# RWKV-7 scan of a two-layer diffusion block: groups of two chunks in place of four, two of them prepared at a time in each direction

## The chip, the cores and the metric

One core of a Trainium2 chip runs the whole program: two layers, one launch. The metric is the device time of an execution in microseconds (us), lower is better. TensorE is PE in the profile, VectorE DVE, ScalarE ACT, GpSimd POOL, and SyncE, which issues most DMAs, SP.

## The reference

Each layer normalizes 512 latent and 256 context tokens, projects them into four groups of mixers (HGRN2, RWKV-7, windowed attention, latent attention), joins them in an output projection and ends with a feed-forward part. The change concerns the RWKV-7 mixer alone, four heads of 64, a recurrence run once forwards and once backwards, over the context first and then over the latent tokens from the state that the context left:

```python
def rwkv7_scan(r, w, k, v, kk, b, s0, reverse):
    def step(S, inp):
        r_t, w_t, k_t, v_t, kk_t, b_t = inp
        sa = jnp.einsum('bhvk,bhk->bhv', S, kk_t)
        S = S * w_t[:, :, None, :] - sa[..., None] * b_t[:, :, None, :] + v_t[..., None] * k_t[:, :, None, :]
        return S, jnp.einsum('bhvk,bhk->bhv', S, r_t)
    xs = tuple(a.transpose(1, 0, 2, 3) for a in (r, w, k, v, kk, b))
    S, o = lax.scan(step, s0, xs, reverse=reverse)
    return o.transpose(1, 0, 2, 3), S

oc_f, sc_f = rwkv7_scan(rc, wc[0], kc, vc, kkc, bc, s0, False)
ol_f, _ = rwkv7_scan(rl, wl[0], kl, vl, kkl, bl, sc_f, False)
oc_b, sc_b = rwkv7_scan(rc, wc[1], kc, vc, kkc, bc, s0, True)
ol_b, _ = rwkv7_scan(rl, wl[1], kl, vl, kkl, bl, sc_b, True)
```

In the last layer the outputs of the context tokens are not needed, only their state.

## The kernel before, in words

The kernel doesn't go token by token. It takes chunks of 64 tokens, 12 in all (8 to 11 are the context, and come first in both directions). Within a chunk, what one token's update does to later ones is a triangular matrix, and the chunk needs its inverse. That inverse, and everything else that doesn't depend on the incoming state, can be made ahead for several chunks; only the state chain goes chunk after chunk.

`rw_dir` (L648) is the generator of one direction. It runs three groups of four chunks. `rw_quad` (L711) prepares a group: it loads the decays W and the keys kkq, makes the operands AR (zeroed halves, L740, then products with W, L741 to L744) and BK (L735, L736), multiplies them into the Gram blocks G for each chunk and masks them (L754), starts the inverse TT as mask plus identity (L763, L766), turns it (TU, TP), turns BK (bkt, L782), and then doubles the size of the inverted blocks in five levels. Each level has three steps with a `yield` behind each: a product of TP with the masked Gram block Gm (L786, on POOL) whose result goes to AP in two halves, one copied by DVE and one by ACT (`pad`, L633); a product of AP with TT, added into TU by DVE (L810) and copied to TP by ACT (L814); and a turn of TU on PE (L328), copied to TT by ACT (L820). The PE products of all helpers stand on L638 (`flip`) and L328 (`turn`).

`rw_chain` (L823) carries the state Z over one chunk: four groups of products (with v, AR·Z, TF, bkt and G), each followed by a copy or an addition on DVE or ACT; it writes the chunk's output into O (L863, L865).

The order of the work is that of the generators: `weave` takes one step of every live generator in turn, both directions, the attention's preparation (`attention_prep`, L1442, half a step at a time) and, in layer 0, the modulation (L425 to L437). Within a direction the group i+1 is prepared step by step beside the chain of group i; the first is prepared alone. Direction 1 starts 10 rounds later. Each engine runs its own instructions in the order so written.

Buffers set a further order. PSUM has two buffers of one bank per direction for the preparation (tag a0 or a1) and one for the chain (c0, c1). In SBUF, G and bkt have two buffers and AR three, all shared by the two directions; v (`vq`), TP and AP exist once per direction.

Of the kernel before, what the change touches and what calls it, by code (L numbers as in the profile page):

```python
# [11 lines left out]
F32 = mybir.dt.float32  # L12
# [5 lines left out]
OP = mybir.AluOpType  # L18
# [204 lines left out]
class Ker:  # L223
# [423 lines left out]

    def rw_dir(s, d, last, g, O, done, both, t0, tp):  # L648
        V = s.V
        s.bp = tp  # L650
# [8 lines left out]
        def values(i):  # L659
            lo = min(order[4 * i:4 * i + 4])  # L660
            for t in range(2):
                h = slice(64 * t, 64 * t + 64)
                s.Q.dma_start(vq[h, :, :, t], s.vd[h, lo:lo + 4].rearrange("p c (h n) -> p c h n", h=2))
        for n, sh in (('TP', [128, 8, 2, 64]), ('AP', [128, 8, 2, 32])):
            z[n], = s.zeroed(tp, sh, f"{n}{d}")
# [12 lines left out]

        def chain(i, Z, zi, ops):
            quad = order[4 * i:4 * i + 4]  # L680
            lo = min(quad)
            for c in range(4):
                Z = yield from s.rw_chain(d, lo, quad[c], last, g, O, done, tp, zi, ops, Z, i == 2 and c == 3)
            if not (last and lo >= 8):
                if lo in both:
                    s.head_squares(O, 1, lo, lo + 4, t0.tile([128, 4, 2, 64], F32, name="Wi"))
                both.add(lo)
            if i < 2:
                values(i + 1)
            return Z  # L690

        cur = yield from prep(0)
        for i in range(3):
            live = {'Z': chain(i, Z, *cur)}
            if i < 2:
                live['cur'] = prep(i + 1)
            res = {}
            while live:
                for n in list(live):
                    try:  # L700
                        next(live[n])
                    except StopIteration as e:
                        res[n] = e.value
                        del live[n]
                yield
            Z, cur = res['Z'], res.get('cur')
            s.rdone += i == 1

    def rw_quad(s, d, lo, last, g, tp, z):

        E, V, S, P = s.E, s.V, s.S, s.P  # L711
        o = 64 * lo
        want = not (last and lo >= 8)
        nm = f"{d}"

        def psa():
            return s.ps("a" + nm, 512, 2)

        def v(x):
            return x[:, :, o:o + 256].rearrange("p t (c n) -> p t c n", c=4)  # L720
        W = tp.tile([128, 2, 4, 64], F32, name="W", bufs=2)
        Wi = tp.tile([128, 2, 4, 64], F32, name="Wi")

# [3 lines left out]
        e = 0 if d else 63  # L727
        We = tp.tile([128, 2, 4, 1], F32, name="We" + nm, bufs=2)
        P.tensor_copy(We, W[:, :, :, e:e + 1])
        AR = z['AR']  # L730
        BK = (s.bp if d else tp).tile([128, 4, 2, 2, 64], F32, name="BK" + nm)
        kv, rv = tp.tile([128, 2, 4, 64], F32, name="kkq", bufs=2), v(g['r'])
        s.Q.dma_start(kv, v(s.rd[:, :2]))
# [11 lines left out]
        yield  # L745
        tp, TP, AP = s.bp, z['TP'], z['AP']
        na = 2 if want else 1

        G = tp.tile([128, 4, 2, 2, 2, 64], F32, name="G", bufs=2)
        for c in range(4):  # L750
# [5 lines left out]
            if c % 2:  # L756
                yield
        S0 = tp.tile([128, 4, 2, 64], F32, name="TT" + nm)

        for t in range(2):  # L760
            for p in range(2):
                h = slice(64 * t, 64 * t + 64)
                (V, P)[p].tensor_tensor(S0[64 * p:64 * p + 64, :, t], G[h, :, 0, p, 0],  # L763
                                s.mskf[h, 1 - d, 0][:, None].to_broadcast([64, 4, 64]), OP.mult)
        sh = [128, 4, 2, 64]
        V.tensor_add(S0, S0, s.id2[:, None, None].to_broadcast(sh))  # L766
        TT = S0
        pt = psa().rearrange("p (x n) -> p x n", x=8)
        for c in range(4):
            s.turn(pt[:, 2 * c:2 * c + 2], S0[:, c])  # L770
        TU = tp.tile([128, 8, 64], F32, name="TU" + nm)
# [5 lines left out]
        for c2 in range(2):  # L777
            pb = psa().rearrange("p (c q h n) -> p c q h n", c=2, q=2, h=2)
            for c in range(2):
                for q in range(2):  # L780
                    s.turn(pb[:, c, q], BK[:, 2 * c2 + c, q])
            S.copy(bkt[:, 2 * c2:2 * c2 + 2], pb)  # L782
        yield
# [5 lines left out]
        for i in range(1, 6):  # L789
            gm, h = gms[i], LVL[i]  # L790
            if i < 5:
                gms[i + 1] = masked(i + 1)

            def half(x):

                return x.rearrange("p x (b e h) -> p x b e h", e=2, h=h)[:, :, :, d]

            def packed(ps):
                return ps[:, :256].rearrange("p (x b h) -> p x b h", x=8, h=h)
            ps = psa()  # L800
            pa = packed(ps)
            for c in range(4):
                s.flip(pa[:, 2 * c:2 * c + 2], lambda p: gm[:, c, p], lambda p: half(TP[:, 2 * c + p]))
            s.pad(AP, ps[:, :256].rearrange("p (x n) -> p x n", x=8), 2)
            yield
            ps = psa()
            p2 = packed(ps)
            for c in range(4):
# [7 lines left out]
            pt = psa().rearrange("p (c t n) -> p c t n", c=4, t=2)  # L816
            for c in range(4):
# [485 lines left out]
    def mixers(s, l, last, xsrc):  # L1303
        V, S, P, Q = s.V, s.S, s.P, s.Q
# [5 lines left out]
        with ExitStack() as wx, ExitStack() as hx:  # L1310
# [7 lines left out]
            with ExitStack() as rx:  # L1318
                rp = rx.enter_context(s.pool("rec", side="right"))
                g = {}  # L1320
# [3 lines left out]
                with ExitStack() as ax:  # L1324
# [11 lines left out]
                    with s.pool("pr", 1, PSUM) as s.pp:  # L1336
# [89 lines left out]
                        done = set()  # L1426
# [15 lines left out]
                def attention_prep(psf):  # L1442
# [13 lines left out]
                    yield from s.swa_prep(l, last, sq, sk, qp, cst, psf, scr)  # L1456
                    while s.rdone < 2:
                        yield

# [4 lines left out]
                with s.pool("b") as tp, s.pool("pb", 1, PSUM) as s.pp:  # L1464
                    done = set(), set()
                    s.rdone, s.nhg = 0, 2
                    wq, wk = bp.tile([128, 768], F32, name="wq"), []
# [5 lines left out]
                    Q.dma_start(s.mskf, s.I['cst'][:, C_MSK:C_MSK + 768].rearrange("p (d h n) -> p d h n", d=2, h=6))  # L1473
                    s.weave(*((s.rw_dir(d, last, g, rwt, *done, tp, tp), 1) for d in range(2)),
                            (attention_prep(s.hps), 0.5), *modulation(tp, scr))
# [526 lines left out]
```

## Time and profile before

| | us |
|---|---|
| median of 3 runs (lowest to highest) | 2707.03 (2705.91 to 2714.2) |
| the profiled execution | 2717.58 |
| its span, mean granted TensorE clock | 2715.7, 0.949 |
| scan stage of layer 0, from 375.2 to 612.2 | 237.0 |
| scan stage of layer 1, from 1698.2 to 1914.5 | 216.3 |

All rows below come from the profiled execution; a time such as 391.16 is counted from the start of its span. The stages' borders are the end of the projection before them and the first product of the attention behind them.

How to read it: the page gives shares over the whole span, and the scan is a sixth of that, so the views of use are the windows (busy time of each engine in a stretch), the groups of instructions within a window (count, busy time, mean, and the idle time of the engine ahead of the group with what ended it), and timelines. "[13.33 <-POOL AR L744]" behind a row says that the engine had been idle for 13.33 us and that POOL's instruction of line 744, which writes AR, ended it. A profile row counts each PE product of the program as two matmuls.

### The profile page before, as it was taken

The numbers are of one execution on the slowest core, as the hardware profiler recorded it, in microseconds if no ns is written. First come the engines' busy times: TensorE is split into PE (matmuls) and PEld (weight loads), VectorE is DVE, ScalarE is ACT, GpSimd is POOL, SyncE is SP. The second block draws the span as 40 slices with busy tenths as digits, with TensorE's granted clock in tenths as the row PEclk, the third lists the DMA queues.
The fourth block names the chain that finished last, engine by engine and source line by source line (L and its number), as shares of the span: only waits on it lengthen the run. The fifth ranks groups of instructions, "written<-read, shape, count | busy, mean of one in ns | idle before, by whom it ended". The sixth has DMA issues, their size and how long they took to land. (4 is left out here: it accounts for less than half of the span.)

```text
span 2715.7 us, 45812 instructions
## 1 busy us (share of the span) xinstructions
PE 2423.3 (89%) x18131; PEld 2004.2 (74%) x18131; DVE 1642.9 (60%) x2846; ACT 1204.1 (44%) x2079; POOL 462.2 (17%) x477
## 2 busy tenths in 40 slices
PE   7998778879998999999999998687898799999994
PEld 3887555666577888888878867466575698899993
DVE  5578945547568654344336696555654667767765
ACT  4644424436733211211237453444564465555653
POOL 1012354412011000000020221643202000000002
PEclk9999789999998999999989999899899799999997
DMA  6222152001044533334322223200201888888885
GB/s 227 79 80 90 61 155 65 16 6 65 21 141 127 161 118 113 119 120 125 109 70 70 87 67 123 75 17 10 71 12 58 281 267 264 280 272 260 262 275 178
DMA packets 183390, 339.21 MB, mean 125 GB/s; under 512 B 25696, under 2 KB 104288, under 8 KB 183168
## 3 DMA queue, kind: packets, MB, share of 16 engines
q1 hardware_dynamic: 176112, 310.38, 36.0%
q0 software_dynamic: 6480, 23.73, 2.5%
q8 instruction: 144, 2.36, 0.4%
q10 hardware_dynamic: 576, 2.10, 0.2%
q14 instruction: 78, 0.64, 0.1%
HBM read 305.88 MB, written 28.84 MB: 123 GB/s over the span
## 5 line engine op out<-in xcount | busy, mean ns | idle before, releaser
L288 PE MATMUL big<-hhi,hiw 128*128 128x512 f32 (+1 forms) x1504 | 525.0, 350 | 10.4 <-ACT hhi L510 4.9
L289 PE MATMUL big<-hlo,hiw 128*128 128x512 f32 (+1 forms) x1504 | 524.0, 349 | 1.5 <-DVE hlo L511 1.5
L290 PE MATMUL big<-hhi,low 128*128 128x512 f32 (+1 forms) x1504 | 520.7, 347 | 5.0 <-DVE low L276 3.9
L275 ACT CAST hiw<-raww 128x512 fp32r<-128x512 f32 (+3 forms) x208 | 158.2, 766 | 559.9 <-PE big L289 358.5
L288 PEld LDWEIGHTS big<-hhi,hiw 128*128 128x128 f32 x1504 | 286.9, 191 | 56.7 <-ACT hhi L510 8.4
L290 PEld LDWEIGHTS big<-hhi,low 128*128 128x128 f32 x1504 | 286.1, 190 | 46.3 <-DVE low L276 5.6
L289 PEld LDWEIGHTS big<-hlo,hiw 128*128 128x128 f32 x1504 | 287.0, 191 | 43.1 <-issue 4.9
L276 DVE TENSOR_TENSOR lom<-rawm,him 128x1024 fp32r<-128x1024 f32 x176 | 215.1, 1224 | 126.2 <-ACT him L275 124.1
L276 DVE TENSOR_TENSOR low<-raww,hiw 128x512 fp32r<-128x512 f32 (+3 forms) x202 | 183.1, 912 | 125.7 <-ACT hiw L275 124.9
L275 ACT CAST him<-rawm 128x1024 fp32r<-128x1024 f32 x176 | 184.2, 1047 | 148.6 <-PE sml L289 62.3
L288 PE MATMUL sml<-xh,him 128*128 128x256 f32 x528 | 151.9, 288 | 0.0
L289 PE MATMUL sml<-xl,him 128*128 128x256 f32 x528 | 149.4, 283 | 0.0
L290 PE MATMUL sml<-xh,lom 128*128 128x256 f32 x528 | 149.4, 283 | 0.0
L276 DVE TENSOR_TENSOR lov<-rawv,hiv 128x1024 fp32r<-128x1024 f32 x88 | 107.6, 1222 | 41.8 <-ACT hiv L275 41.6
L288 PE MATMUL sml<-him,xh 128*128 128x256 f32 x440 | 127.5, 290 | 0.6 <-DVE xl L276 0.6
L289 PE MATMUL sml<-lom,xh 128*128 128x256 f32 x440 | 125.4, 285 | 0.0
L290 PE MATMUL sml<-him,xl 128*128 128x256 f32 x440 | 125.4, 285 | 0.0
L289 PE MATMUL big<-gl,hiw 128*128 128x512 f32 (+1 forms) x352 | 119.5, 339 | 0.0
L288 PE MATMUL big<-gh,hiw 128*128 128x512 f32 (+1 forms) x352 | 118.9, 338 | 0.0
L290 PE MATMUL big<-gh,low 128*128 128x512 f32 (+1 forms) x352 | 118.2, 336 | 0.0
L275 ACT CAST hiv<-rawv 128x1024 fp32r<-128x1024 f32 x88 | 92.4, 1050 | 55.9 <-PE y L290 45.5
L455 DVE SCALAR_TENSOR_TENSOR raww<-raww,cb 128x1024 f32<-128x1024 f32 x56 | 70.3, 1256 | 69.3 <-DMA raww<-in_wadt 68.0
(551 smaller groups left out, 5471.9 us busy)
## 6 DMA issues: line engine op xcount, KB each, us to landing
rawm<-in_m SPq DMA_DIRECT2D x176, 512.0 KB, 5.0
rawv<-in_m SPq DMA_DIRECT2D x88, 512.0 KB, 4.7
raww<-in_wadt SPq DMA_DIRECT2D x56, 512.0 KB, 3.6
raww<-in_w SPq DMA_DIRECT2D x52, 512.0 KB, 3.8
raww<-in_winc SPq DMA_DIRECT2D x92, 256.0 KB, 2.8
raww<-in_wout SPq DMA_DIRECT2D x16, 512.0 KB, 3.8
wadt<-in_wadt SPq DMA_DIRECT2D x16, 512.0 KB, 4.3
raww<-in_w SPq DMA_DIRECT2D x16, 448.0 KB, 3.3
```

The lines of the kernel that those rows point to most:

```text
L275: s.S.copy(hi, src)
L276: (eng or s.V).tensor_sub(lo, src, hi)
L288: s.E.matmul(out, ah, bh, start=start, stop=False)
L289: s.E.matmul(out, ah, bl, start=False, stop=False)
L290: s.E.matmul(out, al, bh, start=False, stop=stop)
L455: V.scalar_tensor_tensor(x, w, 1.0, cb[v], op0=OP.mult, op1=OP.mult, accum_out=m[:, v:v + 1])
```

## The change

The group has two chunks in place of four, so there are six to a direction. `rw_quad` becomes `rw_pair`, with the same steps on operands of half the size and one `yield` fewer. Every direction has two slots, each with its own TP, AP and v and its own single PSUM buffer (tags a00, a01, a10, a11, in place of two buffers for a0 and two for a1). Up to two groups of a direction are prepared at a time, in the two slots, while the chain of a third runs; the second preparation starts 8 rounds after the first, and none runs more than two groups ahead of the chain. AR, G and bkt have five buffers of half the size, shared by both directions; W has three, Wi two. The values of group i+2 are loaded into their slot when chain i has ended. The squares of the outputs are taken for two chunks at a time. Direction 1 starts 5 rounds later in place of 10. In the attention's preparation a wait for the scan's second groups, ahead of the loads of wq and wk, is gone. `rw_chain` is as before.

```diff
-        for _ in range(10 * d):
+        for _ in range(5 * d):
             yield
...
-        vq, = s.zeroed(tp, [128, 4, 2, 2, 64], f"vq{d}")
...
+        slots = []
+        for j in range(2):
+            y = {}
+            for n, sh in (('TP', [128, 4, 2, 64]), ('AP', [128, 4, 2, 32]), ('v', [128, 2, 2, 2, 64])):
+                y[n], = s.zeroed(tp, sh, f"{n}{d}{j}")
+            slots.append(y)
...
         def prep(i):
-            if i == 0:
-                values(0)
-            zi = dict(z, AR=tp.tile([128, 2, 4, 2, 2, 64], F32, name="AR", bufs=3), v=vq)
-            return zi, (yield from s.rw_quad(d, min(order[4 * i:4 * i + 4]), last, g, t0, zi))
+            zi = dict(z, AR=tp.tile([128, 2, 2, 2, 2, 64], F32, name="AR", bufs=5), **slots[i % 2])
+            return zi, (yield from s.rw_pair(d, i % 2, min(order[2 * i:2 * i + 2]), last, g, tp, zi))
...
-            if i < 2:
-                values(i + 1)
+            if i < 4:
+                values(i + 2)
             return Z
 
-        cur = yield from prep(0)
-        for i in range(3):
-            live = {'Z': chain(i, Z, *cur)}
-            if i < 2:
-                live['cur'] = prep(i + 1)
...
+        values(0)
+        values(1)
+        live, ready, nxt, at = {}, {}, 0, -1
+        wait = 0
+        while at < 6:
+            if 'Z' not in live and at + 1 in ready:
+                at += 1
+                live['Z'] = chain(at, Z, *ready.pop(at))
+            while nxt < 6 and sum(n != 'Z' for n in live) < 2 and nxt <= at + 2 and wait <= 0:
+                live[nxt] = prep(nxt)
+                nxt += 1
+                wait = 8 if nxt == 1 else 0
+            wait -= 1
...
-    def rw_quad(s, d, lo, last, g, tp, z):
+    def rw_pair(s, d, slot, lo, last, g, tp, z):
...
-        nm = f"{d}"
+        nm = f"{d}{slot}"
 
         def psa():
-            return s.ps("a" + nm, 512, 2)
+            return s.ps("a" + nm)
...
-        G = tp.tile([128, 4, 2, 2, 2, 64], F32, name="G", bufs=2)
-        for c in range(4):
+        G = tp.tile([128, 2, 2, 2, 2, 64], F32, name="G", bufs=5)
+        for c in range(2):
...
-        bkt = tp.tile([128, 4, 2, 2, 64], F32, name="bkt", bufs=2)
+        bkt = tp.tile([128, 2, 2, 2, 64], F32, name="bkt", bufs=5)
...
-                    while s.rdone < 2:
-                        yield
```

Two places of the order show how the work moves. The first is PE's order in the middle of the scan of layer 0. In the names a1 is a PSUM tile of direction 1's preparation and c0 one of direction 0's chain. Before:

```order
L638 MATMUL a1_5082<-TP10_3463,Gm1_5078 64x64 x8
L638 MATMUL c0_5280<-vq00_3296,bkt_4665 64x128 x2
L638 MATMUL c0_5280<-acc_66,bkt_4665 64x128 x2
L638 MATMUL a1_5110<-AP10_3465,TT1_4993 64x64 x8
L638 MATMUL c0_5300<-vq00_3296,G_4527 64x128 x2
L638 MATMUL c0_5300<-acc_66,G_4527 64x128 x2
L837 MATMUL c0_5300<-Z0_5013,AR_4478 64x64
L328 MATMUL a1_5143<-cst_71,TU1_5004 128x128 x4
L837 MATMUL c0_5300<-Z0_5013,AR_4478 64x64 x3
L638 MATMUL a1_5171<-TP10_3463,Gm1_5080 64x64 x8
L638 MATMUL c0_5331<-vq00_3296,G_4527 64x128 x2
```

And in the changed kernel, where a01 is the preparation of direction 0 in slot 1:

```order
L638 MATMUL a11_5074<-AP110_3403,TT11_5018 64x64 x4
L638 MATMUL a01_5112<-AP010_3306,TT01_5023 64x64 x4
L638 MATMUL c0_5118<-v000_3302,bkt_4048 64x128 x2
L638 MATMUL c0_5118<-acc_66,bkt_4048 64x128 x2
L328 MATMUL a11_5131<-cst_71,TU11_4700 128x128 x2
L328 MATMUL a00_5004<-cst_71,BK00_4839 128x128 x4
L638 MATMUL c1_5136<-acc_66,TF10_5013 64x128 x2
L328 MATMUL a01_5154<-cst_71,TU01_4445 128x128 x2
L638 MATMUL c0_5159<-v000_3302,G_3951 64x128 x2
L638 MATMUL a00_5038<-TP000_3298,Gm00_5034 64x64 x4
L638 MATMUL c0_5159<-acc_66,G_3951 64x128 x2
L844 MATMUL c0_5159<-Z0_4933,AR_3902 64x64 x4
```

Where one preparation (a1, in eights) and one chain (c0) alternated, three preparations (a11, a01, a00, in fours) and the chains of both directions now stand side by side.

The second is POOL's order, where it makes the masked Gram blocks Gm and the next group's AR. The bracket gives the engines and queues whose semaphores an instruction waits for. Before:

```order
L786 TENSOR_TENSOR Gm0_4264<-G_3783,mskf_3290 128x512 [waits PE_49,Pool_49]
L740 MEMSET AR_4478 64x8x128 [waits PE_49]
L742 COPY AR_4478<-kkq_4487 64x8 [waits DMAHW0_49]
L744 TENSOR_TENSOR AR_4478<-W_4479,rwr_111 64x8x64
L740 MEMSET AR_4478 64x8x128 [waits Pool_49]
L742 COPY AR_4478<-kkq_4487 64x8
L744 TENSOR_TENSOR AR_4478<-W_4479,rwr_111 64x8x64
L763 TENSOR_TENSOR TT1_4241<-G_4164,mskf_3290 64x4x64 [waits DVE_49,Activation_49]
```

And in the changed kernel:

```order
L793 TENSOR_TENSOR Gm00_4097<-G_3951,mskf_3290 128x256 [waits PE_49,Pool_49]
L793 TENSOR_TENSOR Gm11_4194<-G_3704,mskf_3290 128x256 [waits PE_49,Pool_49]
L749 MEMSET AR_4147 64x4x128 [waits PE_49]
L751 COPY AR_4147<-kkq_4156 64x4 [waits DMAHW3_49]
L753 TENSOR_TENSOR AR_4147<-W_4148,rwr_111 64x4x64
L749 MEMSET AR_4147 64x4x128 [waits Pool_49]
L751 COPY AR_4147<-kkq_4156 64x4
L753 TENSOR_TENSOR AR_4147<-W_4148,rwr_111 64x4x64
L793 TENSOR_TENSOR Gm00_4231<-G_3951,mskf_3290 128x256 [waits PE_49,Pool_49]
L771 TENSOR_TENSOR TT10_4256<-G_4208,mskf_3290 64x2x64 [waits DVE_49,Activation_49,Pool_49]
```

The instructions of the same kinds act on half as many elements, and those of three preparations (00, 11 and 10) stand between one another; the zeroing of an AR still waits for PE, that is for the chain that used its buffer.

## Rows read from the trace of the kernel before

**Rows 1.** windows of the two scan stages; columns in the first line.
```profile
core 0: us, PE busy (x) PEld busy (x) DVE busy (x) ACT busy (x) POOL busy (x), PEclk, DMA share, GB/s
...
375.20:612.20 237.00, 182.72 (x2377) 132.77 (x2376) 121.58 (x260) 93.48 (x216) 100.29 (x100) 0.90 0.17 47
1698.20:1914.50 216.30, 160.39 (x2201) 123.04 (x2201) 115.00 (x247) 90.63 (x210) 96.88 (x96) 0.90 0.12 32
```

**Rows 2.** timeline of PE at the start of the scan in layer 0: start, us, instruction.
```profile
391.16 4.11 PE L638 MATMUL a<-AR,BK 128*64 128x256 f32 x18 [13.33 <-POOL AR L744]
```

**Rows 3.** timeline of POOL at the same place.
```profile
386.02 1.05 POOL L742 COPY AR<-kkq 64x8 f32<-64x8 f32 x2
...
388.51 2.59 POOL L744 TENSOR_TENSOR AR<-W,rwr 64x512 f32<-64x512 f32 x2
```

**Rows 4.** timeline of PE at the start of the scan in layer 1.
```profile
1714.70 2.62 PE L638 MATMUL a<-AR,BK 128*64 128x128 f32 x22 [1.59 <-issue]
```

**Rows 5.** timeline of all engines at the end of the stage in layer 0.
```profile
611.88 0.29 DVE L863 TENSOR_TENSOR xm<-c,xm 128x128 f32<-128x128 f32 x1 [2.04 <-PE c L837]
...
612.22 1.22 PE L358 MATMUL sc<-xm,wq 128*128 128x512 f32 x1 [0.38 <-DVE xm L863]
```

**Rows 6.** windows of stretches within the stages, columns as in rows 1.
```profile
392.00:447.00 55.00, 48.98 (x493) 29.57 (x490) 37.90 (x62) 26.78 (x53) 32.11 (x31) 0.93 0.31 92
...
531.00:562.00 31.00, 25.57 (x363) 19.29 (x364) 16.66 (x38) 11.69 (x31) 13.57 (x13) 0.94 0.04 10
562.00:592.00 30.00, 23.53 (x370) 19.25 (x366) 14.64 (x34) 13.30 (x33) 7.93 (x7) 0.94 0.05 11
...
1832.00:1863.00 31.00, 25.22 (x385) 19.48 (x383) 17.27 (x40) 12.29 (x34) 13.57 (x13) 1.00 0.04 10
1863.00:1893.00 30.00, 23.46 (x367) 19.08 (x364) 14.85 (x34) 13.38 (x32) 7.94 (x7) 0.94 0.05 11
```

**Rows 7.** groups by form, PE, stage of layer 0: count, busy us, mean ns, idle before.
```profile
L638 PE MATMUL a<-AP,TT 128*64 128x64 f32 x480 | 21.5, 228 | 11.1 <-ACT AP L633 10.2
L328 PE MATMUL a<-cst,TU 128*128 128x128 f32 x120 | 20.1, 291 | 3.0 <-DVE TU L810 2.2
L425 PE MATMUL hg<-wada,scp 128*32 128x512 f32 x32 | 12.6, 605 | 0.6 <-DMA wada<-in_wada 0.6
...
L1202 PE MATMUL hg<-cst,hz 128*128 128x1 f32 x36 | 4.5, 251 | 1.1 <-DVE xm L1395 1.1
...
L1091 PE MATMUL hg<-hq,cst 128*128 128x512 f32 x4 | 3.2, 893 | 0.0
L432 PE MATMUL hg<-cst,scr 128*128 128x128 f32 x8 | 1.9, 300 | 0.9 <-ACT scr L429 0.9
```

**Rows 8.** groups by form, PE, stage of layer 1.
```profile
L1202 PE MATMUL hg<-cst,hz 128*128 128x1 f32 x28 | 4.8, 295 | 10.2 <-ACT hz L1198 9.1 <-DVE xm L1395 1.1
...
L1091 PE MATMUL hg<-hq,cst 128*128 128x512 f32 x4 | 2.3, 645 | 0.6 <-DVE scr L1093 0.6
L1216 PE MATMUL hg<-cst,mr 128*128 128x128 f32 x6 | 1.8, 439 | 0.0
```

**Rows 9.** timeline of DVE where a chain runs alone, layer 0.
```profile
599.49 0.29 DVE L853 TENSOR_TENSOR Z<-c,Z 128x128 f32<-128x128 f32 x1 [1.11 <-PE c L638]
...
604.58 0.29 DVE L853 TENSOR_TENSOR Z<-c,Z 128x128 f32<-128x128 f32 x1 [1.21 <-PE c L638]
```

**Rows 10.** groups by form, DVE, stage of layer 0.
```profile
L633 DVE COPY AP<-a 64x256 f32<-64x256 f32 x30 | 12.3, 414 | 22.9 <-PE a L638 22.9
...
L633 DVE COPY acc<-c 64x128 f32<-64x128 f32 x36 | 10.1, 280 | 19.3 <-PE c L837 9.9 <-PE c L638 9.1
```

**Rows 11.** groups by form, ACT, stage of layer 0.
```profile
L633 ACT COPY AP<-a 64x256 f32<-64x256 f32 x30 | 11.0, 367 | 17.9 <-DVE AP L633 17.3 <-DVE mod L436 0.3
L633 ACT COPY acc<-c 64x128 f32<-64x128 f32 x36 | 9.3, 260 | 18.7 <-DVE acc L633 18.2
```

**Rows 12.** the line L663 (the loads of v), both layers.
```profile
L663 SPq DMA_DIRECT2D vq<-vd x24: 573/608/1155, 376.7 to 1862.4; - x24
...
DMA to landing us min/median/max: 2.7/3.0/6.0
```

More of the change, by code (lines that the diff above doesn't have):

```diff
@@ L646, in zeroed, with rw_dir @@
         return r
-    def rw_dir(s, d, last, g, O, done, both, t0, tp):
+    def rw_dir(s, d, last, g, O, done, both, tp):
         V = s.V
-        s.bp = tp
-        for _ in range(10 * d):
+        for _ in range(5 * d):
             yield
@@ L656, in rw_dir @@
         z = {}
-        vq, = s.zeroed(tp, [128, 4, 2, 2, 64], f"vq{d}")
[L659 to L665, printed above, removed]
         for i, n in enumerate(('RP', 'UP')):
@@ L670, in rw_dir, with values @@
             z[n] = x.rearrange("p (a b n) -> p a b n", a=2, b=2)
-        order = (FWD_CH, BWD_CH)[d]
+        slots = []
[4 more added lines that the diff above has]
+            slots.append(y)
+        order = (FWD_CH, BWD_CH)[d]
+        def values(i):
+            lo = min(order[2 * i:2 * i + 2])
+            for t in range(2):
+                h = slice(64 * t, 64 * t + 64)
+                s.Q.dma_start(slots[i % 2]['v'][h, :, :, t], s.vd[h, lo:lo + 2].rearrange("p c (h n) -> p c h n", h=2))
@@ L681, in chain @@
-            lo = min(quad)
-            for c in range(4):
-                Z = yield from s.rw_chain(d, lo, quad[c], last, g, O, done, tp, zi, ops, Z, i == 2 and c == 3)
+            pair = order[2 * i:2 * i + 2]
+            lo = min(pair)
+            for c in range(2):
+                Z = yield from s.rw_chain(d, lo, pair[c], last, g, O, done, tp, zi, ops, Z, i == 5 and c == 1)
             if not (last and lo >= 8):
                 if lo in both:
-                    s.head_squares(O, 1, lo, lo + 4, t0.tile([128, 4, 2, 64], F32, name="Wi"))
+                    s.head_squares(O, 1, lo, lo + 2, tp.tile([128, 2, 2, 64], F32, name="Wi", bufs=2))
@@ L709, in rw_quad @@
-    def rw_quad(s, d, lo, last, g, tp, z):
+            if i < 4:
+                values(i + 2)
+            return Z
+        values(0)
[11 more added lines that the diff above has]
+            wait -= 1
+            for n in list(live):
+                try:
+                    next(live[n])
+                except StopIteration as e:
+                    if n == 'Z':
+                        Z = e.value
+                    else:
+                        ready[n] = e.value
+                    del live[n]
+            yield
+            if at == 5 and not live:
+                break
@@ L713, in rw_quad @@
         want = not (last and lo >= 8)
-        nm = f"{d}"
+        nm = f"{d}{slot}"
         def psa():
-            return s.ps("a" + nm, 512, 2)
+            return s.ps("a" + nm)
         def v(x):
-            return x[:, :, o:o + 256].rearrange("p t (c n) -> p t c n", c=4)
-        W = tp.tile([128, 2, 4, 64], F32, name="W", bufs=2)
-        Wi = tp.tile([128, 2, 4, 64], F32, name="Wi")
+            return x[:, :, o:o + 128].rearrange("p t (c n) -> p t c n", c=2)
+        W = tp.tile([128, 2, 2, 64], F32, name="W", bufs=3)
+        Wi = tp.tile([128, 2, 2, 64], F32, name="Wi", bufs=2)
         s.Q.dma_start(W, v(s.rd[:, 2 + 2 * d:4 + 2 * d]))
@@ L727, in rw_quad @@
         e = 0 if d else 63
-        We = tp.tile([128, 2, 4, 1], F32, name="We" + nm, bufs=2)
+        We = tp.tile([128, 2, 2, 1], F32, name="We" + nm, bufs=2)
         P.tensor_copy(We, W[:, :, :, e:e + 1])
         AR = z['AR']
-        BK = (s.bp if d else tp).tile([128, 4, 2, 2, 64], F32, name="BK" + nm)
-        kv, rv = tp.tile([128, 2, 4, 64], F32, name="kkq", bufs=2), v(g['r'])
+        BK = tp.tile([128, 2, 2, 2, 64], F32, name="BK" + nm)
+        kv, rv = tp.tile([128, 2, 2, 64], F32, name="kkq", bufs=2), v(g['r'])
         s.Q.dma_start(kv, v(s.rd[:, :2]))
@@ L745, in rw_quad @@
         yield
-        tp, TP, AP = s.bp, z['TP'], z['AP']
+        TP, AP = z['TP'], z['AP']
         na = 2 if want else 1
-        G = tp.tile([128, 4, 2, 2, 2, 64], F32, name="G", bufs=2)
-        for c in range(4):
+        G = tp.tile([128, 2, 2, 2, 2, 64], F32, name="G", bufs=5)
+        for c in range(2):
             pg = psa().rearrange("p (q h a n) -> p q h a n", q=2, h=2, a=2)
@@ L755, in rw_quad @@
                             s.mg[:, d, :, :64 * na][:, :, None].to_broadcast([128, 2, 2, 64 * na]), OP.mult)
-            if c % 2:
-                yield
-        S0 = tp.tile([128, 4, 2, 64], F32, name="TT" + nm)
+        yield
+        S0 = tp.tile([128, 2, 2, 64], F32, name="TT" + nm)
         for t in range(2):
@@ L763, in rw_quad @@
                 (V, P)[p].tensor_tensor(S0[64 * p:64 * p + 64, :, t], G[h, :, 0, p, 0],
-                                s.mskf[h, 1 - d, 0][:, None].to_broadcast([64, 4, 64]), OP.mult)
-        sh = [128, 4, 2, 64]
+                                s.mskf[h, 1 - d, 0][:, None].to_broadcast([64, 2, 64]), OP.mult)
+        sh = [128, 2, 2, 64]
         V.tensor_add(S0, S0, s.id2[:, None, None].to_broadcast(sh))
         TT = S0
-        pt = psa().rearrange("p (x n) -> p x n", x=8)
-        for c in range(4):
+        pt = psa()[:, :256].rearrange("p (x n) -> p x n", x=4)
+        for c in range(2):
             s.turn(pt[:, 2 * c:2 * c + 2], S0[:, c])
-        TU = tp.tile([128, 8, 64], F32, name="TU" + nm)
+        TU = tp.tile([128, 4, 64], F32, name="TU" + nm)
         S.copy(TU, pt)
@@ L774, in rw_quad @@
         yield
-        bkt = tp.tile([128, 4, 2, 2, 64], F32, name="bkt", bufs=2)
[L777 to L782, printed above, removed]
+        bkt = tp.tile([128, 2, 2, 2, 64], F32, name="bkt", bufs=5)
+        pb = psa().rearrange("p (c q h n) -> p c q h n", c=2, q=2, h=2)
+        for c in range(2):
+            for q in range(2):
+                s.turn(pb[:, c, q], BK[:, c, q])
+        S.copy(bkt, pb)
         yield
@@ L798, in packed @@
             def packed(ps):
-                return ps[:, :256].rearrange("p (x b h) -> p x b h", x=8, h=h)
+                return ps[:, :128].rearrange("p (x b h) -> p x b h", x=4, h=h)
             ps = psa()
             pa = packed(ps)
-            for c in range(4):
+            for c in range(2):
                 s.flip(pa[:, 2 * c:2 * c + 2], lambda p: gm[:, c, p], lambda p: half(TP[:, 2 * c + p]))
-            s.pad(AP, ps[:, :256].rearrange("p (x n) -> p x n", x=8), 2)
+            s.pad(AP, ps[:, :128].rearrange("p (x n) -> p x n", x=4), 2)
             yield
@@ L807, in rw_quad @@
             p2 = packed(ps)
-            for c in range(4):
+            for c in range(2):
                 s.flip(p2[:, 2 * c:2 * c + 2], lambda t: TT[:, c, t], lambda t: AP[:, 2 * c + t])
@@ L815, in rw_quad @@
             yield
-            pt = psa().rearrange("p (c t n) -> p c t n", c=4, t=2)
-            for c in range(4):
+            pt = psa()[:, :256].rearrange("p (c t n) -> p c t n", c=2, t=2)
+            for c in range(2):
                 s.turn(pt[:, c], TU[:, 2 * c:2 * c + 2])
@@ L1465, in mixers @@
                     done = set(), set()
-                    s.rdone, s.nhg = 0, 2
+                    s.nhg = 2
                     wq, wk = bp.tile([128, 768], F32, name="wq"), []
@@ L1473, in mixers @@
                     Q.dma_start(s.mskf, s.I['cst'][:, C_MSK:C_MSK + 768].rearrange("p (d h n) -> p d h n", d=2, h=6))
-                    s.weave(*((s.rw_dir(d, last, g, rwt, *done, tp, tp), 1) for d in range(2)),
+                    s.weave(*((s.rw_dir(d, last, g, rwt, *done, tp), 1) for d in range(2)),
                             (attention_prep(s.hps), 0.5), *modulation(tp, scr))
```

12 lines of the change are left out of this document (removed).

## The prediction

> **What bounds the kernel now.** I read first the windows by stage, since a mean over 2,716 us hides this stage. The RWKV scan fills 237.0 us in layer 0 and 216.3 us in layer 1 [rows 1]. PE is the busiest engine there, with 182.72 and 160.39 us, so it is idle for 23% and 26% of the time; DVE, ACT and POOL are busy for half or less. PE is not full, and no other engine is: the stage is a chain of hand-overs with gaps.
>
> Next come the borders, in the timelines. At the start PE does nothing for the scan until 391.16, after 13.33 us without work, released by POOL's AR [rows 2]; POOL comes to the first AR copy at 386.02, after its zeroing, and ends the products with r at 388.51 + 2.59 = 391.10 [rows 3]. In layer 1 the first G product starts at 1714.70 [rows 4]. So the fronts last 16.0 us (from 375.2) and 16.5 us (from 1698.2). At the end, the output addition of the last chunk starts at 611.88 and the first product of the following stage at 612.22, released by it [rows 5]. Whatever the stage saves, the program therefore saves.
>
> Then the stretches in the middle [rows 6]. In 531 to 592 and 1832 to 1893 one direction prepares a group of four while the other runs its chain: two streams of work. PE is busy for 25.57 + 23.53 and 25.22 + 23.46 us of 61 each, together 97.78 of 122, or 80%. The stage of layer 0 has 2,377 matmuls, of which 80 belong to the four other groups below, so a pair (its preparation and chain) has 2,297 / 12 = 191. The two stretches have 363 + 370 + 385 + 367 = 1,485 matmuls, or 7.8 pairs. A pair thus takes **15.7 us** now, of which PE works **12.6 us**. By contrast, in 392 to 447 both directions prepare and the projections of the attention run beside them: PE is busy for 48.98 of 55.00 us, **89%** [rows 6].
>
> What ends PE's gaps, by groups: 11.1 us before AP·TT, nearly all on ACT's half of the AP copy, and 3.0 us before the turns of TU, mostly on DVE's addition [rows 7]. These waits are for a level's own last step. They can be filled only by matmuls of another stream.
>
> **The change, part by part.** The useful arithmetic is unchanged: the same matmuls in the same shapes, 191 per pair. What changes is how many streams can stand between two waits. Each direction has slots for two preparations, and the five shared AR, G and bkt allow three of these beside two chains. The order on PE shows this: rows of a11, a01, a00, c0 and c1 alternate where there were a1 and c0.
>
> *Time of a pair.* The price of full overlap isn't in the trace. From below it is PE's own work, 12.6; from above, with nothing gained, 15.7 as now; something worse is a rival below. I take the nearest row, the stretch of 392 to 447, where several independent streams give 89%: 12.6 / 0.89 = **14.2 us**, and 170.4 us for 12 pairs.
>
> *Front.* POOL zeroes as many bytes as before, in more pieces (five half-size AR for three). Its work from the first copy to the end of the products with r, 5.1 us [rows 3], is on half-size operands: about 2 us less. Layer 0: 14. In layer 1 the first G row stands behind other work as well; I take 1 us less, 15.5. Bounds: nothing gained, or 3 us each.
>
> *Other PE work of the stage.* Layer 0: 12.6 + 4.5 + 3.2 + 1.9 = 22.2 us [rows 7], at 0.89 this is 25. Layer 1: 2.3 + 1.8 [rows 8] is 4.1, so 5; its 4.8 us of L1202 lie within the front.
>
> *Context chunks of layer 1* write no output. The stage's PE time differs by 182.72 - 160.39 = 22.3 us, of which the other work explains 22.2 - 8.9 = 13.3; the remaining 9.0, at 0.89, is 10 us off.
>
> *Drain.* A chain by itself goes 5.1 us per chunk (Z added at 599.49 and at 604.58 [rows 9]). Now over two chunks of one direction end the stage alone; with 5 rounds of offset in place of 10 I take one, 5 us. Bounds 3 and 10.
>
> *More instructions.* A group of four becomes two of two, which adds 17 instructions on DVE, 22 on ACT and some 15 on POOL for each old group, six groups to a layer. The fixed part of one comes from two sizes: DVE needs 414 ns for 256 elements and 280 for 128 [rows 10], so 146 ns fixed; ACT 367 and 260 [rows 11], 153 ns. That is 102 x 0.146 = 15 us on DVE and 132 x 0.153 = 20 us on ACT per layer. I cost both at nothing, since they are covered by PE: in the middle stretches DVE works 63.4 us for 7.8 pairs, 8.2 per pair, and would have 9.4 of 14.2; ACT 50.7, 6.5, and 8.2. If that cover went, they would add 35 us per layer, or 2.9 per pair.
>
> *DMAs.* SP gets twice as many issues for W, kkq and v. The v of pair i+2 is fetched when chain i has ended; it has chain i+1 to land in, two chunks or 10 us at least, against 3.0 us usually and 6.0 at most [rows 12]. A refill waits for the chain's last read and can hold kkq and W of another group behind it in SP's queue; these are asked for early in a preparation that is itself one of three. No cost taken; up to 1 us per refill (8 a layer) is inside the range. *PSUM.* A preparation has one bank in place of two per direction, so G's second chunk waits for the first one's eviction; the other streams cover that. *The removed wait* for the groups' count cost nothing, as the transfers behind it weren't waited for.
>
> **Sum.** Layer 0: 14 + 170.4 + 25 + 5 = 214.4, 22.6 less than 237.0. Layer 1: 15.5 + 170.4 - 10 + 5 + 5 = 185.9, 30.4 less than 216.3. Together **-53.0 us** against the profiled run's 2717.6, so 2664.6; that run is 10.6 us above the median shown, so I predict **2654** for the median. With p as the time of a pair, the change is -53.0 + 24 (p - 14.2): zero at p = 16.4.
>
> **Rivals.**
>
> *A, PE nearly saturated* (p 12.6 to 13.3). For: pieces are half as long, so more of them fit in a gap. Against: all streams share in-order engines, with DVE then at 9.4 of 12.6. Gives 2616 to 2632.
>
> *B, the streams don't overlap as written* (p 14.8 to 16). The order on each engine is fixed ahead, so a late AP copy stops the rows behind it, although their operands are ready; POOL, with 100.29 / 12 = 8.4 us in a pair [rows 1] before its extra instructions, feeds every stream. In that case the change does not do what its words say. At 15.7 only fronts and drain gain: -17 us, 2690.
>
> *C, slower: twice as many hand-overs, each exposed as now.* Place: AP·TT and the turns of TU, whose gaps are 14.1 us per layer [rows 7], 1.2 per pair. If other streams fill no more than today, a second set brings p to 16.9: +12 us, 2719. It decides from p = 16.4. If all the fixed parts on DVE and ACT came in series as well, p = 18.6 and 2760. For: the copies' fixed 146 and 153 ns are over a third of the small ones. Against: in 392 to 447 the same hand-overs with more streams left PE only 11% idle. The Trainium skill, page VectorE: DVE Perf Modes, section on the TRN2 errata, speaks against this change: a large tile pays the latency between instructions once, many small ones each time, and it advises 512 elements or more, where the change goes from 512 and 256 to 256 and 128. The rows agree that a fixed part is there [rows 10]. By that rule alone the sum would be the 2760 just named; by the idle time of DVE and ACT in the middle [rows 6] it is the forecast's.
>
> **How the numbers follow.** Forecast, p 13.3 to 14.8, 2632 to 2668: 0.47. A: 0.17. B, up to 2699: 0.24. C: 0.12. The range is 2612 to 2692, which leaves out C, the end of B and a little below A: 0.2. A measurement of this kernel tells 0.3%, or 8 us, from no change. The forecast, A and B are below 2699: 0.88 faster; C is split into 0.04 the same and 0.08 slower.
>
> **What would show it.** Right: stages of about 214 and 186 us; PE at 88% or more of the middle; the gap before AP·TT well under 11 us; first scan product some 2 us earlier; DVE busy 15 us longer and ACT 20 per layer. B: PE at 80% in the middle, gaps before AP·TT and TU's turns as long in sum as now. C: those gaps doubled. A: PE over 94%. Wrong altogether: a new releaser at the head of PE's gaps, such as POOL's masked G, or a kkq or v transfer.

## The result, and the profile after

The changed kernel takes 2662.93 us, the median of 4 runs (2658.14 to 2667.17), against 2706.47 before (4 runs, 2702.29 to 2714.2). The ratio is **0.9835, interval 0.9807 to 0.9864**, or 44 us less by the medians. The forecast was 2654, with 2612 to 2692 as its range. The profiled execution took 2658.14 us, its span is 2656.0.

The windows of the two stages in the kernel after, and of an early stretch in layer 1 (columns in the first line):

```profile
core 0: us, PE busy (x) PEld busy (x) DVE busy (x) ACT busy (x) POOL busy (x), PEclk, DMA share, GB/s
376.05:586.70 210.65, 181.17 (x2377) 128.23 (x2376) 123.51 (x365) 112.29 (x351) 113.40 (x196) 0.96 0.19 53
1664.40:1857.40 193.00, 159.48 (x2200) 120.57 (x2200) 122.38 (x351) 108.14 (x343) 108.39 (x188) 0.93 0.13 36
...
1682.00:1730.00 48.00, 39.44 (x483) 27.87 (x479) 39.50 (x97) 28.28 (x91) 37.98 (x59) 0.87 0.11 32
```

The middles alone, from the first G product to the last product of a preparation:

```profile
389.70:576.00 186.30, 171.93 (x2242) 120.86 (x2242) 116.39 (x343) 104.27 (x334) 100.51 (x167) 0.98 0.16 44
1679.50:1845.00 165.50, 144.40 (x2018) 107.64 (x2020) 112.72 (x319) 98.51 (x324) 96.60 (x159) 0.96 0.10 26
```

The stages last 210.65 and 193.0 us, where they took 237.0 and 216.3 [rows 1]: 26.4 and 23.3 us less, together 49.7. (The two profiled executions differ by 59.4 us; the other 10 lie outside the change. The one before, 2717.58 us, is slower than its four timed runs and the one after is the fastest of its four, so the 49.7 is rather high: the medians give 44.) PE is busy for as long as before (181.17 against 182.72, 159.48 against 160.39), so nearly the whole gain, 24.8 and 22.4 us, is idle time of PE that has gone. In the middles PE is now busy for 171.93 / 186.3 = 92% and 144.40 / 165.5 = 87%.

The groups of PE in the stage of layer 0 after (count, busy us, mean ns, idle before):

```profile
L638 PE MATMUL a<-AR,BK 128*64 128x256 f32 x192 | 33.2, 422 | 18.8 <-POOL AR L753 18.0 <-DVE G L763 0.8
...
L638 PE MATMUL a<-AP,TT 128*64 128x64 f32 x480 | 28.1, 229 | 1.2 <-ACT AP L633 0.7
...
L328 PE MATMUL a<-cst,TU 128*128 128x128 f32 x120 | 24.7, 294 | 0.7 <-DVE TU L817 0.6
```

The gap before AP·TT went from 11.1 us to 1.2, and that before TU's turns from 3.0 to 0.7 [rows 7]. What is left stands before the G products, 18.0 us on POOL's AR, of which 11.06 is the front, as PE's timeline has it:

```profile
389.74 1.97 PE L638 MATMUL a<-AR,BK 128*64 128x256 f32 x8 [11.06 <-POOL AR L753]
```

POOL's timeline at the same place:

```profile
386.77 0.50 POOL L751 COPY AR<-kkq 64x4 f32<-64x4 f32 x2
...
388.17 1.51 POOL L753 TENSOR_TENSOR AR<-W,rwr 64x256 f32<-64x256 f32 x2
```

The front is shorter as worked out: its chain from the first AR copy to the end of the products with r took 5.1 us [rows 3] and takes 388.17 + 1.51 - 386.77 = 2.9 now.

At the end of the stage, the last product of a preparation and the first of the next stage (PE's timeline):

```profile
576.05 0.44 PE L328 MATMUL a<-cst,TU 128*128 128x128 f32 x2
...
586.72 2.85 PE L358 MATMUL sc<-xm,wq 128*128 128x512 f32 x8 [0.38 <-DVE xm L870]
```

Before, the same two rows stood at 590.87 and 612.22 [the second in rows 5]:

```profile
590.87 0.66 PE L328 MATMUL a<-cst,TU 128*128 128x128 f32 x4
```

So the drain, chains alone, shrank from 21 to 11 us in layer 0, and in layer 1 from 23 to 11 (the last product of a preparation starts at 1891.79 before and at 1846.77 after). Of the 49.7 us some 4 come from the fronts, 23 from the drains, and 23 from the middles. In the drains PE's work went with the time: it was busy for 12.91 of the 20.2 us from 592 on, and is for 7.25 of 10.2.

### The profile page after: what moved, and what is told of

Same layout as the page of the kernel before. It is cut to its first block, busy times and chain, and to the rows that moved or that the text cites. A ratio compares the mean times of both kernels' runs of the same rounds, so it can differ in the third digit from the quotient of the medians.

```text
span 2656.0 us, 46639 instructions
## 1 busy us (share of the span) xinstructions
PE 2411.9 (91%) x18131; PEld 1991.5 (75%) x18131; DVE 1649.4 (62%) x3055; ACT 1240.9 (47%) x2348; POOL 487.5 (18%) x665
```

## The experiments

The first runs, up to the offset of the directions, take parts of the change away. All ratios are to the kernel before, run beside them on the same chip.

**The split alone.** One preparation at a time per direction, and the old counts of buffers:

```diff
-..., name="AR", bufs=5)        -..., name="G", bufs=5)        -..., name="bkt", bufs=5)
+..., name="AR", bufs=3)        +..., name="G", bufs=2)        +..., name="bkt", bufs=2)
-            while nxt < 6 and sum(n != 'Z' for n in live) < 2 and nxt <= at + 2 and wait <= 0:
+            while nxt < 6 and sum(n != 'Z' for n in live) < 1 and nxt <= at + 2 and wait <= 0:
```

> The groups of two chunks are kept, but only one is prepared at a time in each direction, and AR, G and bkt have 3, 2 and 2 buffers, as many as before (of half the size). Theory (the gain is the third, fourth and fifth stream that fill PE's gaps): the gain is gone and the fixed parts of the smaller copies show, about 2700 to 2730 us, with the gap before AP.TT back at 10 us or more per layer. Rival 1 (the shorter pieces alone make the gain, since each hand-over holds PE for half as long): within 10 us of the changed kernel, about 2663. Rival 2 (front, drain and offset make it): about 2680 to 2690.

Measured: 2817.82 us, ratio 1.0386 (1.0357 to 1.0414). Both rivals fall, and the price of the split is far above the theory's own. The windows of the stages, and then what PE waits for in layer 0 behind the front (us in total, times, longest):

```profile
377.50:670.50 293.00, 225.22 (x2376) 152.77 (x2376) 130.65 (x365) 116.44 (x351) 114.74 (x196) 0.81 0.14 38
1751.50:2017.60 266.10, 201.55 (x2200) 143.87 (x2200) 124.27 (x351) 112.89 (x343) 114.15 (x196) 0.79 0.10 26
```

The waits:

```profile
PE a L638 <- ACT TT L827: 14.7, 29, 1.0
PE a L638 <- POOL AR L753: 9.3, 7, 1.8
PE a L638 <- ACT AP L633: 6.0, 16, 0.9
```

The stages take 293.0 and 266.1 us, 106 us more than before, 4.4 us per pair. Most of that is PE's busy time: it is busy for 84 us more over both layers for the same products (225.22 us against 182.72 in layer 0), and idle for 22 us more. The granted clock is 0.81 against 0.90 in layer 0 [rows 1], means over stretches at 2.4 and at 1.2 GHz. A matmul of TP·Gm takes 274 ns on the mean, in the changed kernel 228, by PE's groups of layer 0:

```profile
L638 PE MATMUL a<-TP,Gm 128*64 128x64 f32 x480 | 36.4, 274 | 19.6 <-ACT TT L827 14.7 <-ACT bkt L789 3.4 <-POOL Gm L793 0.6
```

The same group in the kernel before:

```profile
L638 PE MATMUL a<-TP,Gm 128*64 128x64 f32 x480 | 22.2, 230 | 3.3 <-issue 2.4 <-ACT TP L633 0.5 <-POOL hz L1094 0.3
```

The gap that grew is not the one before AP·TT (6.0 us on the AP copy) but this one, from 3.3 to 19.6 us, and 18.1 us of it wait for the copies of TT and bkt. Neither is an operand of TP·Gm. Both copies empty the PSUM bank into which the product then writes: a preparation has one bank in `rw_pair`, where it had two. So this run differs from the kernel before by the halved pieces and by the lost bank (and by the offset of 5 rounds), and no run gives the bank back: the 4% are the price of both together. In the changed kernel the other streams cover this wait, too: 1.0 us on TT's copy in layer 0, 3.1 in layer 1.

How much of the longer busy time is the clock, and how much that the products come in fours in place of eights, was not separated. (The buffers hold as many groups as before, hence as many streams, but half as many chunks.)

**One preparation at a time, with the five buffers kept** (the last pair of lines of the diff above alone):

> One preparation at a time in each direction, but the five buffers of AR, G and bkt kept, so that both directions can prepare beside both chains: four streams in place of five. Theory: most of the gain stays, 2670 to 2690. If it is the two slots of a direction that matter and not the count of streams over both: near 2700 or above.

Measured: 2676.32 us, 0.9869 (0.9841 to 0.9897). As the theory had it: the buffers, which let both directions prepare beside both chains, carry most of the gain. The second slot is worth at most the rest; in the runs' times the two intervals overlap. In the profile the stages last 217.2 and 198.35 us, 12 more than with both:

```profile
374.70:591.90 217.20, 185.71 (x2376) 128.68 (x2376) 128.78 (x365) 113.92 (x352) 113.58 (x196) 0.95 0.19 51
1674.05:1872.40 198.35, 167.43 (x2200) 124.33 (x2200) 119.04 (x351) 110.54 (x344) 110.17 (x188) 0.91 0.13 35
```

**Three buffers, and four**, with two slots (in both, `bufs=5` of AR, G and bkt replaced):

> Two slots per direction as in the change, but three buffers of AR, G and bkt in place of five, so that three groups in all are in flight, chains among them. Theory: between the changed kernel and split_alone, 2685 to 2710. If the buffers don't decide and the slots do: within 8 us of the changed kernel.

> The changed kernel with four buffers of AR, G and bkt in place of five: one stream fewer. three buffers gave 2742, five 2663. Theory (each stream fills gaps until PE is full, so the steps get smaller): 2680 to 2700. If the fifth buffer is one too many, as PE is full with four: within 8 us of 2663.

Measured: three 2741.97 us, 1.0111 (1.0085 to 1.0136), slower than before; four 2681.02, 0.9891 (0.9874 to 0.9908). The slope is steeper than expected at three and as expected at four. By buffers the series is 2742, 2681, 2663 for three, four and five: each adds less. With three, PE is busy in the three stretches from 445 to 595 for 80% to 82%:

```profile
445.00:495.00 50.00, 40.65 (x525) 29.30 (x522) 27.27 (x82) 26.95 (x81) 25.51 (x45) 1.00 0.12 33
...
545.00:595.00 50.00, 41.00 (x515) 29.91 (x512) 24.92 (x75) 21.14 (x71) 21.40 (x38) 0.93 0.04 9
```

That is the share of the kernel before [rows 6], with shorter pieces and two slots: the pieces give nothing by themselves (with one bank for each preparation, as above).

**The offset of the directions**, 10 rounds as before, and none (`range(10 * d)`, `range(0 * d)`):

> The changed kernel with the second direction 10 rounds behind in place of 5. Theory: the offset touches front and drain only, so 2660 to 2670, the same within what can be told. Rival 2 (the smaller offset makes a part of the gain): 2675 or more.

> The changed kernel with both directions starting together. An offset of 10 rounds cost some 17 us against 5. If the loss is that the second direction ends later and its last chunks stand alone: 2655 to 2663. If what matters is that the directions are out of step, so that they don't need POOL and the buffers at the same time: 2670 or more.

Measured: with 10, 2684.42 us, 0.9897 (0.9868 to 0.9926); with none 2667.61, 0.9839 (0.9821 to 0.9857), not told from the change's 5. The first theory of the 10 was missed and its rival 2 held: with the old offset the change is worth 27 us against the kernel before run beside it, in place of 44, so the smaller offset makes a part of the gain, and it touches more than the ends. The stages with 10:

```profile
371.70:592.00 220.30, 186.10 (x2376) 131.28 (x2376) 124.43 (x365) 113.69 (x351) 113.80 (x196) 0.92 0.18 51
1676.70:1883.70 207.00, 169.31 (x2200) 124.96 (x2200) 120.68 (x351) 110.33 (x343) 108.43 (x188) 0.89 0.13 33
```

They are 9.7 and 14.0 us longer than with 5. PE's busy time has 15 of these 24 us, at a lower clock (0.92 and 0.89, against 0.96 and 0.93), and its idle time 9. In layer 0 the drain is 3 us longer (its last product of a preparation is at 578.65, the next stage at 592.0), and the waits for POOL's AR after the front are 10.5 us where the changed kernel has 6.9. With none, the time lies between the ranges of the two theories; in the profile the stage of layer 0 is as long as with 5 (210.8 us) and that of layer 1 is 198.5, 5.5 longer, so whether being out of step is worth anything stays open. Why the G products wait longer with 10 was not followed further.

**The hand-overs measured**: each copy into AP made twice, in the changed kernel, in the kernel before, and the changed kernel unaltered beside them:

```diff
             s.pad(AP, ps[:, :128].rearrange("p (x n) -> p x n", x=4), 2)
+            s.pad(AP, ps[:, :128].rearrange("p (x n) -> p x n", x=4), 2)
```

> The changed kernel once more, unaltered, beside the others of this call: 2655 to 2670. It gives the base for the runs beside it.

> The changed kernel, with each copy of the product TP.Gm into AP made twice on both engines, one after the other (120 more copies of 0.28 us on DVE and as many of 0.26 us on ACT over both layers). Theory (the other streams cover a late hand-over): 12 us or less above the changed kernel. Rival (the hand-overs are in series for PE): 33 us or more above it, since each AP.TT then starts at least 0.28 us later.

> The same doubling in the kernel before (60 more copies of 0.41 us on DVE, 0.37 us on ACT). Theory: with two streams it is exposed, 15 to 25 us above the kernel before. If two streams cover it as well: within 8 us.

Measured: unaltered 2663.72 us, 0.9831 (0.9801 to 0.9862); doubled 2679.73, 0.9888 (0.9856 to 0.992), 16 us more; before, doubled, 2745.84, 1.0135 (1.0101 to 1.0169), 35 us more. The cover is neither whole nor absent: 120 late hand-overs cost 0.13 us each in the changed kernel, 60 cost 0.59 us each in the kernel before, more than I gave them and more than the copy itself lasts (0.41). A copy made twice also keeps DVE and ACT from the other streams, so these are prices of a longer hand-over and not of waiting alone.

PE's group before AP·TT with doubled copies, changed kernel, layer 0:

```profile
L638 PE MATMUL a<-AP,TT 128*64 128x64 f32 x480 | 27.7, 228 | 1.9 <-ACT AP L633 1.6
```

The same in the kernel before, layer 0:

```profile
L638 PE MATMUL a<-AP,TT 128*64 128x64 f32 x480 | 22.6, 235 | 12.3 <-ACT AP L633 12.3
```

And in layer 1, with the window of that stage:

```profile
L638 PE MATMUL a<-AP,TT 128*64 128x64 f32 x480 | 22.2, 239 | 19.2 <-ACT AP L633 19.2
```

```profile
1703.90:1941.70 237.80, 171.60 (x2200) 131.65 (x2200) 127.76 (x277) 100.73 (x239) 95.25 (x96) 0.84 0.10 29
```

In layer 0 the gap hardly grew (from 11.1 us), and the stage is 8.7 us longer. Most of the price lies in layer 1: its stage is 21.5 us longer, the gap went from 9.0 to 19.2 us, and PE is busy for 171.60 us in place of 160.39, at a clock of 0.84 in place of 0.90.

**POOL at the front.** W and kkq loaded first, zeroing behind the first step of a preparation:

```diff
-                y[n], = s.zeroed(tp, sh, f"{n}{d}{j}")
+                y[n] = tp.tile(sh, F32, name=f"{n}{d}{j}0")
...
+            steps = s.rw_pair(d, i % 2, min(order[2 * i:2 * i + 2]), last, g, tp, zi)
+            next(steps)
+            if i < 2:
+                for n in ('TP', 'AP', 'v'):
+                    s.P.memset(slots[i][n], 0.0)
+                values(i)
+            yield
+            return zi, (yield from steps)
...
-        values(0)
-        values(1)
```

> The changed kernel, with W and kkq of the first groups loaded ahead of v, and the zeroing of TP, AP and v written behind the first step of each slot's first preparation. Theory (POOL's zeroing and the order of the loads hold the first G product back): it starts 3 to 5 us earlier in each layer, 6 to 10 us less than the changed kernel. Rival (the exponentials and the loads themselves set it): within 3 us.

Measured: 2660.96 us, 0.9813 (0.9779 to 0.9847), within 3 us of the unaltered one. Not the rival's reason, though: the first G product comes 12.4 us after the stage's start in layer 0 (13.7 with the change) and 9.8 in layer 1 (15.1), but the time comes back. PE's next G product in layer 0 waits again, since POOL now does the zeroing that is left between the products of AR:

```profile
386.82 1.97 PE L638 MATMUL a<-AR,BK 128*64 128x256 f32 x8 [9.81 <-POOL AR L758]
391.62 0.70 PE L638 MATMUL a<-AR,BK 128*64 128x256 f32 x2 [2.83 <-POOL AR L758]
```

POOL's timeline there:

```profile
386.82 0.53 POOL L681 MEMSET v<- 128x512 f32 x1
387.28 1.09 POOL L754 MEMSET AR<- 64x512 f32 x2
388.45 0.73 POOL L750 TENSOR_TENSOR BK<-Wi,rwk 128x256 f32<-128x256 f32 x1
...
389.87 1.70 POOL L758 TENSOR_TENSOR AR<-W,rwr 64x256 f32<-64x256 f32 x2
```

**POOL's work on AR.** The halves that are zeroed are never written, so five tiles can be zeroed once and kept. In a first version, `ar_zeroed_once`, the tiles simply rotated, and a preparation could write an AR whose chain was still to be issued, so that some chains used another group's AR:

> The changed kernel with five AR tiles that are zeroed at their first use only, since the zeroed halves are never written again: 28 POOL instructions of 0.52 us fewer over both layers, and the waits for PE in POOL's queue move from the zeroing to the first product. Theory (POOL's AR is what PE still waits for ahead of the G products): 5 to 12 us less than the changed kernel. Rival (PE is full in the middle, so POOL's time there is hidden): within 4 us.

It took 2646.29 us, 0.9758 (0.9739 to 0.9777), with fewer waits than the computation needs, so it tells only that POOL's share is not nothing. The second version gives an AR back by a list:

```diff
-            zi = dict(z, AR=tp.tile([128, 2, 2, 2, 2, 64], F32, name="AR", bufs=5), **slots[i % 2])
+            zi = dict(z, AR=s.free.pop(0), **slots[i % 2])
...
+            s.free.append(zi['AR'])
             if i < 4:
                 values(i + 2)
...
-            while nxt < 6 and ... and wait <= 0:
+            while nxt < 6 and ... and wait <= 0 and s.free:
...
-            P.memset(AR[h, :, :, 1 - p], 0.0)
```

> The five AR tiles are zeroed once and kept, as in ar_zeroed_once, but a group takes one only from a list to which the chain that used it has given it back, so that every chain reads its own AR. POOL has 28 instructions of 0.52 us fewer over both layers. Theory (POOL's work on AR is what PE still waits for, at the start and ahead of later G products): 5 to 15 us less than the changed kernel. Rival (hidden, PE being full in the middle): within 4 us.

Measured: **2649.76 us, 0.9774 (0.9752 to 0.9796)** over 5 runs, ahead of the changed kernel as of the one before. What PE waits for behind the front in layer 0, with the change:

```profile
PE a L638 <- POOL AR L753: 6.9, 7, 1.4
PE a L328 <- DVE TT L774: 1.8, 2, 1.1
PE c L638 <- ACT acc L633: 1.5, 4, 0.7
```

With the kept AR:

```profile
PE a L638 <- POOL AR L757: 1.8, 2, 1.6
PE c L638 <- ACT acc L633: 1.6, 4, 0.7
PE a L638 <- DVE G L767: 1.5, 2, 0.8
```

Its stages and two stretches of the middle, in the windows:

```profile
376.70:580.50 203.80, 179.36 (x2376) 128.05 (x2376) 122.96 (x365) 111.74 (x352) 107.45 (x182) 0.94 0.19 55
1657.80:1847.00 189.20, 157.91 (x2201) 120.69 (x2201) 118.90 (x351) 109.27 (x344) 103.08 (x174) 0.94 0.14 37
447.00:500.00 53.00, 50.44 (x704) 36.11 (x703) 35.04 (x103) 30.21 (x100) 28.41 (x49) 0.97 0.23 63
500.00:550.00 50.00, 48.24 (x718) 37.07 (x716) 31.11 (x103) 29.65 (x102) 24.62 (x38) 1.00 0.06 14
```

POOL's AR was the longest wait left, 6.9 us, and is 1.8 now. PE is busy for 50.44 + 48.24 of 103 us, 96%. The stages are 203.8 and 189.2 us long. In the changed kernel PE is busy for 91% of the same two stretches:

```profile
447.00:500.00 53.00, 49.61 (x657) 34.44 (x657) 29.84 (x93) 27.26 (x90) 25.51 (x45) 1.00 0.20 55
500.00:550.00 50.00, 43.85 (x615) 32.71 (x612) 30.47 (x92) 27.45 (x90) 27.70 (x49) 1.00 0.08 19
```

The version also starts a preparation only when an AR has come back, so POOL's shorter work and this order were not told apart.

## Why the prediction was right, point by point

*The mechanism held.* Gaps of two streams are filled when five run; PE works as long as before and is idle for 47 us less. The run with the split alone, which differs from the changed kernel in the streams only and takes 155 us more, shows that the count of streams does it, and the runs with three, four and five buffers that the shared buffers set that count. Not all of the gain is the streams': the offset of the directions, which the prediction counted in the drain alone, is worth some 17 to 21 us of it when it goes back to 10.

*The time of a pair* was right through two errors that cancel. PE's work per pair was put at 12.6 us by counting matmuls in stretches that hold too few of the G products. A pair has 16 of these (192 / 12), and the stretch from 531 to 592, taken for 3.8 pairs, has those of three, in PE's groups of the kernel before:

```profile
L638 PE MATMUL a<-TP,Gm 128*64 128x64 f32 x160 | 7.5, 233 | 1.1 <-issue 1.1
L638 PE MATMUL a<-AR,BK 128*64 128x256 f32 x48 | 7.5, 463 | 3.1 <-POOL AR L744 2.9 <-DVE G L754 0.2
```

A G product takes PE three times as long as one of the other group (7.5 / 48 against 7.5 / 160 us), so this is a part of what was missing. From the whole stage after, the work is (181.17 - 22.2) / 12 = 13.2 us. PE's share was put at 89%, and is 92% in the middle of layer 0. That the two cancel there is luck. Behind the front the stage of layer 0 takes 197.0 us, where the terms gave 170.4 + 25 + 5 = 200.4.

*Layer 1 was mis-sized.* The terms gave 170.4 us behind the front, it took 177.9. The windows behind the fronts, and the first stretch of layer 0:

```profile
389.74:586.70 196.96, 179.68 (x2364) 126.81 (x2364) 120.85 (x358) 107.00 (x343) 100.51 (x167) 0.98 0.15 42
1679.49:1857.40 177.91, 153.87 (x2172) 115.16 (x2172) 118.58 (x339) 101.55 (x334) 96.60 (x159) 0.96 0.09 24
392.00:447.00 55.00, 52.53 (x550) 32.96 (x550) 40.58 (x107) 33.29 (x99) 37.62 (x58) 0.95 0.23 66
```

The term that was too small is PE's work per pair. In layer 1 the terms hold 12 x 12.6 - 9.0 + 4.1 = 146.3 us of it, and PE is busy for 153.9; the idle time, 24.0 us, is what the terms gave (170.4 - 146.3 = 24.1). In layer 0 the work was too small by nearly as much (12 x 12.6 + 22.2 = 173.4 against 179.7 us), but PE is idle for 17.3 us there, where the terms left 200.4 - 173.4 = 27.0. The credit for the context chunks held: PE's times of the two stages differ by 181.17 - 159.48 = 21.7 us, where 22.3 were taken. Layer 1 lacks the cover at its start: in the stretch 1682 to 1730, shown above, PE is busy for 82% (DVE is for as long, 39.50 us), in layer 0 from 392 to 447 for 96%, with the modulation's products beside the scan's. That these are the reason is read from the windows; no run took it apart. Layer 0 came out 3.8 us better than its terms and layer 1 7.1 worse: 49.7 in place of 53.0.

*Fronts* took 13.7 and 15.1 us, against 14 and 15.5. *The drain's* idle part is 3.0 us (10.2 less 7.25), against 5. *The added instructions*: ACT has 18.8 us more in layer 0 (20 forecast), DVE only 1.9 (15 forecast), in part for the reason below. That they were covered holds in the main, not wholly: a hand-over made longer by one more copy still costs 0.13 us. *PSUM*: the single bank was seen for the G products alone; it is TP·Gm that waits for it when the other streams are missing.

*Rival C* named the right danger and the wrong place and price. Where only two streams run, the stages take 106 us more, not 28 (1.2 us for each of 24 pairs), at TP·Gm and in PE's busy time more than at AP·TT, and the lost bank has a part in it; with five streams it does not decide. Its dearest case was added up too low: 18.6 is 15.7 + 2.9, the fixed parts without the second set of hand-overs; with it p is 16.9 + 2.9 = 19.8, or 2788. *Rival B's* sign, PE at 80%, shows with three buffers, but the time there is 2742, not 2690, and no run shows that a late AP copy is the reason. *A's* sign, PE above 94%, shows in two stretches once POOL's AR work is shortened; its time, 2632 or less, was not reached. The Trainium skill, page VectorE: DVE Perf Modes, section on the TRN2 errata, says that many small tiles pay a latency each time, and the split alone is indeed slower. That such a latency is the cause isn't shown there, though: DVE is busy for 130.65 us in layer 0 against 121.58 [rows 1], 9 of 56 us. With five streams the halved pieces are faster all the same.

## What to carry to other kernels

If PE is idle between short dependent steps, count the independent streams and the buffers that limit them before shortening any step: halving the pieces paid here through the additional streams that half-size buffers allowed in the same memory, and without these, with one PSUM bank less for each preparation, it cost 4%. (Groups of four with more buffers were not run.) When the releaser of a wait is none of the product's operands, look for the buffer that it empties. Groups half as long also halve what runs alone at the end. When PE is above 90%, look at the engine that feeds the first product of each group: here it was POOL, zeroing what was zero already. And try the offset between two like directions: 10 rounds in place of 5 took away more than a third of the gain.

## What was not expected of the hardware

DVE's operations between tiles in SBUF lost half their time with half their size, the copies from PSUM did not. Two such groups of DVE, layer 0, after:

```profile
L633 DVE COPY AP<-a 64x128 f32<-64x128 f32 x60 | 16.0, 278 | 10.5 <-PE a L638 10.3
...
L771 DVE TENSOR_TENSOR TT<-G,mskf 64x128 f32<-64x128 f32 x24 | 10.8, 451 | 0.3
```

and the second in the kernel before:

```profile
L763 DVE TENSOR_TENSOR TT<-G,mskf 64x256 f32<-64x256 f32 x12 | 10.9, 909 | 0.1
```

The product for TT takes 451 ns for 128 elements, before it took 909 for 256; the copy into AP takes 278 against 414 [rows 10]. The fixed part that I read off two PSUM copies and gave to all of DVE's instructions is theirs alone in these rows; why the others have none isn't settled by them, since they also run beside POOL.
